# Branch sum by accumulating stores, gate weights in y's memory, last weights in free memory

## The chip, the cores and the metric

One core of one Trainium2 chip runs the kernel. The metric is device time in microseconds for one execution, and less is better. TensorE (PE) multiplies matrices, VectorE (DVE), ScalarE (ACT) and GpSimd (POOL) work on tiles in on-chip memory, and SyncE (SP) issues most of the transfers; each engine runs its own instructions in order and waits for the others through semaphores.

## The reference

One decoder layer with S = D = 1024 and three token mixers side by side:

```python
h = rms_norm(x, g_norm)
proj = h @ w_in            # q, k, v, indexer, latent, cross and gate columns
o_a = dsa_attention(...)   # sparse: indexer scores, the 256 best keys per query, 8 heads of 64
o_b = causal_attention(...)  # latent attention, 8 heads
o_m = cross attention into 256 memory tokens, 4 heads
ys = stack([o_a * silu(z_a), o_b * silu(z_b), o_m * silu(z_m)])
branch = einsum('nbsw,nwd->nbsd', ys, w_branch)
merged = einsum('bsnd,nbsd->bsd', sigmoid(gate_logits), branch)
out = x + merged @ w_out
```

## The kernel before, in words

All products are wanted at fp32 accuracy from faster operands, so each matrix is held as a rounded part and its remainder (hi and lo, names ending in h and l), and each product is three matmuls: `mm3`, lines 273 to 275. Weights come in as a raw tile (name ending in r) by a DMA of SP (`wload`, L258), are cast on ACT (L241), and the remainder is taken on DVE (L244). `hTh` and `hTl` hold the normed, transposed input all the time.

The order of the stages is: projections and norms; cross attention; latent attention; the indexer, which scores keys for the top-k; then the three branches and the output product. The top-k search goes on beside what follows: `run_topk(i_, n)` puts pieces of it on DVE and ACT behind a given instruction. `branch(n, ...)` does one mixer: for four pieces w it makes the z product (`z_part`, 48 matmuls, names z0w for the weights), loads the mixer's output (`osb`), multiplies and splits it into `yh`, `yl`; then for eight column tiles d and two row halves j it makes 12 matmuls into a bank `br`, loads the gate tile `tg` (the tanh that was computed earlier and stored in `s_tg`), and calls `emit`. Branch 2 uses `emit_b`, which stores (tg + 1) * br into the sum `s_acc` in DRAM. Branch 1 uses `emit_m`, which adds to what is there: it loads the tile of `s_acc` first. Branch 0 (`emit_a`, at the end) adds the last part and keeps the sum on chip for the output product.

Around branch 2 and 1 stand `qkv(p)`, p = 0 to 3, which make the sparse attention's queries, keys and values, and `early`, which does three of branch 0's four z products ahead of time and stores them in `s_z`. In the program the order is branch 2 with qkv(0), branch 1 with qkv(1), the first early z, qkv(2), the next, qkv(3), the transposes of head 0's keys (`k_prep`, PE bank `akt`, results `akh`, `akl`), the third early z. Then comes the sparse attention: per head and query group G, `q_prep` transposes queries (bank a_3q for G = 3), the scores go into banks a_3S, softmax gives a_3p, which is transposed (a_3pt) and multiplied with the values (`avst`). Between these a `Filler` runs gate products f_d_j (24 matmuls each, weights f_d_a, result tanh `fo`, stored to `s_tg`). The table PREA says how many products of three matmuls the filler does ahead of the scores of the first units, and what is left runs behind the last unit. Then branch 0 with its last z product (z0w_0, memory pool `w5`), and the output product with weights `wo`, loaded in `pre_wo` at the eighth piece of branch 0.

The order within an engine comes from the tile scheduler. Memory comes from pools that stack on a left and a right side; a new pool that lies in the memory of a closed one makes its first writers wait for the old one's last users.

Of the kernel before, what the change touches and what calls it, by code (L numbers as in the profile page):

```python
# [12 lines left out]
FR = mybir.dt.float32r  # L13
# [3 lines left out]
ALU = mybir.AluOpType  # L17
# [4 lines left out]
S = 1024  # L22
D = 1024
P = 128
# [11 lines left out]
WSB = [1]  # L36
WSI = [1]
PREB = (0, 0, 0, 16)
PREA = (0, 0, 0, 0)
NFQ = 2  # L40
PFQ = 4
NZG = 3
# [53 lines left out]
def f(ap):  # L96
    return ap.bitcast(F32)
# [3 lines left out]
def hybrid_kernel(  # L101
# [5 lines left out]
    nc = tc.nc  # L107
    x, mem, out = x[0], mem[0], out[0]
# [15 lines left out]
    def ps_t(nm, dt=F32):  # L124
        return pp.tile([P, 512], dt, tag="tp", name=nm, bufs=NTP)
# [14 lines left out]
    ident = cp.tile([P, P], F32, name="ident")  # L140
# [475 lines left out]
    with ExitStack() as ph:  # L616
# [31 lines left out]
        with ExitStack() as ph2:  # L648
# [64 lines left out]
            for h in range(4):  # L713
                tp = ps_t(f"kmt{h}")
# [614 lines left out]
    with w3s as ph:  # L1329
# [5 lines left out]
        def acc_at(d, j):  # L1335
            return s_acc[d * P:(d + 1) * P, j * 512:(j + 1) * 512]
# [6 lines left out]

        def emit_m(d, j, tg, pb):
            ac = wk.tile([P, 512], F32, tag="ac", name=f"am{d}_{j}", bufs=3)
            nc.sync.dma_start(ac, acc_at(d, j))
            nc.vector.scalar_tensor_tensor(out=tg, in0=tg, scalar=1.0, in1=pb, op0=ALU.add, op1=ALU.mult)
            i_ = nc.vector.tensor_tensor(ac, tg, ac, op=ALU.add)
            nc.gpsimd.dma_start(acc_at(d, j), ac)
            run_topk(i_, 2.6)  # L1350

        def qkv(p):
# [62 lines left out]
                nc.sync.dma_start(f(qs)[:, 4 * j:4 * j + 4, :],  # L1415
                                  s_qa[p][j].rearrange("p (t h d) -> p t h d", t=4, h=2)[:, :, hh, :])

        def k_prep(p, hh):
            if (p, hh) in st:
                return  # L1420
            h = 2 * p + hh
            kd = st["k", p]
            kTh = hd.tile([P, S], FR, tag="kTh", name=f"akh{h}")
            kTl = hd.tile([P, S], FR, tag="kTl", name=f"akl{h}")
            for j in range(2):
                tp = ps_t(f"akt{h}_{j}")
                for i in range(4):
                    nc.tensor.transpose(tp[:, i * P:(i + 1) * P],
                                        kd[:, 4 * j + i, hh].rearrange("p a d -> p (a d)"), ident)
                cs = slice(j * 512, (j + 1) * 512)  # L1430
                nc.scalar.copy(kTh[:, cs], tp)
                nc.vector.tensor_tensor(kTl[:, cs], tp, f(kTh[:, cs]), op=ALU.subtract)
            st[p, hh] = (kTh, kTl)

        ws[:] = WSG

        def early(a, b):
# [5 lines left out]
        early(0, 1)  # L1443
        qkv(2)
        ys.close()
        hd = hds.enter_context(tc.tile_pool(name="aheads", bufs=2, side="right", reuse_waits="tile"))
        load_k(0)
        load_q(0, 0)
        load_q(0, 1)
        early(1, 2)  # L1450
        qkv(3)
        k_prep(0, 0)
        early(2, NZG)

    run_topk(None, 99)
# [1 line left out]


    with ExitStack() as ph:
        wk2 = ph.enter_context(tc.tile_pool(name="awork2", bufs=2, reuse_waits="tile"))  # L1460
        vp = ph.enter_context(tc.tile_pool(name="avals", bufs=2, reuse_waits="tile"))
        for t in range(2):
            m = msk[t] = vp.tile([P, (t + 1) * P], BF, name=f"msk{t}", bufs=1)
            nc.gpsimd.memset(m, 0.0)
            nc.gpsimd.affine_select(out=m[:, t * P:(t + 1) * P], in_=m[:, t * P:(t + 1) * P],
                                    pattern=[[-1, P]], compare_op=ALU.is_ge, fill=NEG, base=0,
                                    channel_multiplier=1)
        zero_tiles(wk2, 1)
        pv_bufs[:] = PVA

        def load_gen(p):
            yield 1
            if p:
                load_k(p)
            vst = vp.tile([P, NT, 4, 64], FR, tag="vst", name=f"avst{p}")
            st["v", p] = (vst, [None, None])
            for j in range(2):
                nc.sync.dma_start(f(vst).rearrange("p t e d -> p (t e d)")[:, 1024 * j:1024 * j + 1024], s_va[p][j])
            yield 1
            if p:  # L1480
                load_q(p, 0)
            yield 1
            if p:
                load_q(p, 1)

        def q_prep(p, hh, G):
            h = 2 * p + hh
            qs = st["q", p, hh]
            nm = f"a{h}_{G}"
            tp = ps_t(nm + "q", FR)  # L1490
            for b in range(2):
                nc.tensor.transpose(tp[:, b * P:(b + 1) * P],
                                    qs[:, 2 * G + b], identr)
            qT = wk2.tile([P, 256], FR, tag="aqT", name=nm + "qT")
            nc.vector.tensor_copy(qT, f(tp)[:, 0:256])
            return qT

        def s_mm(u, b):
            (p, hh, G), qT = u.unit, u.q
            kTh, kTl = st[p, hh]  # L1500
            t = 2 * G + b
            n = (t + 1) * P
            q_ = qT[:, b * P:(b + 1) * P]
            mx = sm.tile([P, 2], F32, tag="mxb", name=f"{u.nm}mx{b}")
            pt = p_tile(wk2, G, f"{u.nm}p{b}")
            ch = s_chunks(n)
            for c, (k0, w, m) in enumerate(ch):
                sp = ps_s(f"{u.nm}S{b}_{c}")
                nc.tensor.matmul(sp[:, 0:w], q_, kTh[:, k0:k0 + w], start=True, stop=False)
                nc.tensor.matmul(sp[:, 0:w], q_, kTl[:, k0:k0 + w], start=False, stop=True)  # L1510
                masked(pt, sp, m, msk[t][:, k0:k0 + m], k0, mx, c)
            return pt, min_of(mx, ch), n

        def scores(p, hh, G, q):
            u = Scores(f"a{2 * p + hh}_{G}", wk2, G, s_mm)
            u.unit, u.q = (p, hh, G), q
            return u

        def pv(p, hh, G, sc):
            vst, oa = st["v", p]  # L1520
            if oa[hh] is None:
                oa[hh] = wk2.tile([P, S], F32, tag="oa", name=f"oa{p}", bufs=1) if hh == 0 else oa[0]
            o_ = oa[hh]

            def store():
                nc.sync.dma_start(s_o[0][P * p:P * p + P, :], o_)
            return PV(sc.nm, wk2, G, sc, hh, lambda kt: vst[:, kt, 2 * hh:2 * hh + 2].rearrange("p e d -> p (e d)"),
                      o_[64 * hh:64 * hh + 64, 2 * G * P:2 * (G + 1) * P],
                      store if hh == 1 and G == GORD[-1] else None)

        fp = ph.enter_context(tc.tile_pool(name="afill", bufs=1, reuse_waits="tile"))
        ws[:] = WSQ
        attention(load_gen, k_prep, q_prep, scores, pv, pool_filler(fp, take_jobs("F", NFA), FWA, FBB), PFA, PREA, GENA, LDA)

# [4 lines left out]
    with ExitStack() as ph:  # L1539
# [6 lines left out]
        wpa = ph.enter_context(tc.tile_pool(name="w6a", bufs=1, reuse_waits="tile"))  # L1546
        with ExitStack() as ph2:
            wkz = ph2.enter_context(tc.tile_pool(name="zwork5", bufs=2, reuse_waits="tile"))
            wpool = ph2.enter_context(tc.tile_pool(name="w5", bufs=2, reuse_waits="tile"))
            yp = ph2.enter_context(tc.tile_pool(name="y5", bufs=1, reuse_waits="tile"))  # L1550
            wk = ph2.enter_context(tc.tile_pool(name="gwork5", bufs=2, reuse_waits="tile"))

            def emit_a(d, j, tg, pb):
                ac = wk.tile([P, 512], F32, tag="ac", name=f"ac{d}_{j}", bufs=3)
                nc.sync.dma_start(ac, s_acc[d * P:(d + 1) * P, j * 512:(j + 1) * 512])
                i_ = nc.vector.scalar_tensor_tensor(out=tg, in0=tg, scalar=1.0, in1=pb, op0=ALU.add, op1=ALU.mult)  # L1556
                split_low(i_)
                nc.gpsimd.tensor_tensor(ac, ac, tg, op=ALU.add)  # L1558
                nc.scalar.activation(hTh[d][j], ac, AF.Copy, scale=0.25)
                late.append((d, j, ac))  # L1560

            late = []

            def split_low(after):
                for d, j, ac in late:
                    with tc.issue_after(after.ins) if after is not None else ExitStack():
                        nc.vector.scalar_tensor_tensor(out=hTl[d][j], in0=ac, scalar=0.25, in1=f(hTh[d][j]),
                                                       op0=ALU.mult, op1=ALU.subtract)
                late.clear()

            assert all((0, d) in gates_done for d in range(NK))
            pool_raw[:] = PRF
            pre = []

            def pre_wo(after, pe):
                pre.append(0)
                if len(pre) == PRW:
                    pool_raw[:] = [1, 8]
                    wo_load(wpa, 0)
                    pool_raw[:] = list(PRF)  # L1580

            ws[:] = WSF
            branch(0, C_ZA, wpool, wkz, yp, s_o[0], emit_a, pre_wo, 4, wk, ZB5, OB5)
            ws[:] = WSO
            split_low(None)
# [44 lines left out]
```

## Time and profile before

| what | value |
|---|---|
| three runs | 1434.66, 1435.96, 1440.41 us, median 1435.96 |
| profiled execution | 1439.17 us, span 1437.4 us, mean granted clock of PE 0.987 |
| PE busy | 1369.2 us, 95% of the span, 7440 matmul rows |
| DVE busy | 965.6 us, 67% |
| ACT busy | 680.8 us, 47% |
| POOL busy | 200.7 us, 14% |

The span is the time between the first and the last instruction of the profiled execution. Busy shares say how much of it an engine worked; a wait row says which engine waited at which line and what came last before it went on; a window row gives the busy time of all engines between two times, with the clock that PE was granted as a share of full speed.

### The profile page before, as it was taken

The numbers are of one execution on the slowest core, as the hardware profiler recorded it, in microseconds if no ns is written. First come the engines' busy times: TensorE is split into PE (matmuls) and PEld (weight loads), VectorE is DVE, ScalarE is ACT, GpSimd is POOL, SyncE is SP. The second block draws the span as 40 slices with busy tenths as digits, with TensorE's granted clock in tenths as the row PEclk, the third lists the DMA queues.
The fourth block names the chain that finished last, engine by engine and source line by source line (L and its number), as shares of the span: only waits on it lengthen the run. The fifth ranks groups of instructions, "written<-read, shape, count | busy, mean of one in ns | idle before, by whom it ended". The sixth has DMA issues, their size and how long they took to land.

```text
span 1437.4 us, 20940 instructions
## 1 busy us (share of the span) xinstructions
PE 1369.2 (95%) x7440; PEld 1171.5 (82%) x7440; DVE 965.6 (67%) x2450; ACT 680.8 (47%) x1464; POOL 200.7 (14%) x240
## 2 busy tenths in 40 slices
PE   7999999899999999999999999799889999969998
PEld 5998888788988889877897897598878888857787
DVE  5845436678888751688868787877778788836411
ACT  6635433366666651465645554333246566623200
POOL 3050004510102000000022003112300000003200
PEclk9999999999999999999999999999999999989999
DMA  7411212311121130112408523853163341266622
GB/s 247 132 45 59 92 37 86 116 54 41 49 68 40 45 126 23 30 44 81 132 37 271 153 74 138 282 153 125 52 183 97 95 125 60 73 191 186 208 97 73
DMA packets 155992, 151.65 MB, mean 106 GB/s; under 512 B 38256, under 2 KB 115056, under 8 KB 155888
## 3 DMA queue, kind: packets, MB, share of 16 engines
q1 hardware_dynamic: 149328, 127.77, 29.9%
q0 software_dynamic: 5984, 20.45, 3.7%
q10 hardware_dynamic: 576, 2.10, 0.4%
q8 instruction: 58, 0.95, 0.3%
q14 instruction: 46, 0.38, 0.1%
HBM read 103.63 MB, written 46.66 MB: 105 GB/s over the span
## 4 chain that ended last, share of the span: by engine, by line
PE 59%; DVE 14%; issue 8%; DMA 7%; ACT 7%; POOL 3%; SPq 0%; ACTq 0%; DVEq 0%; POOLq 0%
PE f L273 5%; PE f L274 5%; PE f L275 5%; DVE kdj L1039 3%; ACT kag L1045 2%; PE o L275 2%; PE o L273 2%; PE o L274 2%; DVE idx L1233 1%; DMA s_acc<-am 1%; PE ixps L274 1%; PE ixps L275 1%; PE ixps L273 1%; PE b_3pt L462 1%; PE qmps L275 1%
## 5 line engine op out<-in xcount | busy, mean ns | idle before, releaser
L1045 ACT ACTIVATE kag<-idx,kaT 128x896 bf16<-128x896 f32 (+2 forms) x96 | 82.8, 862 | 51.2 <-DVE kaT L1066 44.9
L1039 DVE TENSOR_SCALAR_CACHE_REDUCE kdj<-idx,kdT 128x1024 bf16<-128x1024 f32 (+2 forms) x96 | 92.3, 962 | 0.7
L273 PE MATMUL f<-hTh,f_0h 128*128 128x512 f32 x184 | 78.8, 428 | 2.6 <-ACT fo L365 1.9
L273 PE MATMUL f<-hTh,f_1h 128*128 128x512 f32 x184 | 76.4, 415 | 0.0
L275 PE MATMUL f<-hTh,f_0l 128*128 128x512 f32 x184 | 74.1, 403 | 0.0
L275 PE MATMUL f<-hTh,f_1l 128*128 128x512 f32 x184 | 74.0, 402 | 0.0
L274 PE MATMUL f<-hTl,f_1h 128*128 128x512 f32 x184 | 73.8, 401 | 0.0
L274 PE MATMUL f<-hTl,f_0h 128*128 128x512 f32 x184 | 73.7, 400 | 0.0
L1558 POOL TENSOR_TENSOR ac<-ac,tg 128x512 f32<-128x512 f32 x16 | 22.2, 1397 | 277.9 <-DVE tg L1556 264.3
L1600 DVE TENSOR_TENSOR xr<-o,xr 128x512 f32<-128x512 f32 x16 | 11.1, 691 | 65.1 <-PE o L275 64.2
L1227 ACT ACTIVATE irl<-is 128x512 f32<-128x512 f32 (+1 forms) x80 | 37.8, 528 | 15.6 <-DVE idx L1233 11.9
L365 ACT ACTIVATE fo<-f 128x512 f32<-128x512 f32 x48 | 28.8, 599 | 33.9 <-PE f L275 30.0
L273 PEld LDWEIGHTS f<-hTh,f_0h 128*128 128x128 f32 x184 | 34.8, 189 | 9.5 <-ACT fo L365 4.1
L1233 DVE SCALAR_TENSOR_TENSOR idx<-irl,wi,idx 128x1024 f32<-128x1024 f32 (+5 forms) x42 | 40.3, 959 | 2.6 <-ACT irl L1227 0.9
L275 PEld LDWEIGHTS f<-hTh,f_0l 128*128 128x128 f32 x184 | 35.0, 190 | 6.4
L275 PEld LDWEIGHTS f<-hTh,f_1l 128*128 128x128 f32 x184 | 34.8, 189 | 6.3
L274 PEld LDWEIGHTS f<-hTl,f_1h 128*128 128x128 f32 x184 | 34.9, 190 | 4.5
L273 PEld LDWEIGHTS f<-hTh,f_1h 128*128 128x128 f32 x184 | 34.9, 189 | 4.2
L274 PEld LDWEIGHTS f<-hTl,f_0h 128*128 128x128 f32 x184 | 35.1, 191 | 3.8
L1225 PE MATMUL is<-kih,iqT 128*128 128x512 f32 (+1 forms) x80 | 30.1, 381 | 2.8 <-ACT irl L1227 2.4
L273 PE MATMUL z<-hTh,z0w_0h 128*128 128x512 f32 x40 | 18.2, 456 | 13.2 <-ACT z0w_0h L241 9.2
L1174 DVE TENSOR_SCALAR wi<-ixps 128x8 f32<-128x8 f32 x8 | 1.3, 166 | 42.0 <-ACT xi L1172 42.0
(1238 smaller groups left out, 4772.9 us busy)
## 6 DMA issues: line engine op xcount, KB each, us to landing
s_tg<-fo SPq DMA_DIRECT2D x48, 256.0 KB, 2.0
tg<-s_tg SPq DMA_DIRECT2D x48, 256.0 KB, 3.9
f_0r<-in_w_in_dram SPq DMA_DIRECT2D x23, 256.0 KB, 3.0
f_1r<-in_w_in_dram SPq DMA_DIRECT2D x23, 256.0 KB, 3.0
xx<-in_x_dram SPq DMA_DIRECT2D x8, 512.0 KB, 7.2
osb<-s_o SPq DMA_DIRECT2D x16, 256.0 KB, 3.1
s_acc<-ab POOLq DMA_DIRECT2D x16, 256.0 KB, 5.0
am<-s_acc SPq DMA_DIRECT2D x16, 256.0 KB, 4.0
```

Source lines behind the costliest of these rows:

```text
L273: nc.tensor.matmul(ps, ah, bh, start=start, stop=False)
L274: nc.tensor.matmul(ps, ah, bl, start=False, stop=False)
L275: nc.tensor.matmul(ps, al, bh, start=False, stop=stop)
L365: nc.scalar.activation(o, ps, AF.Tanh, scale=0.5)
L462: nc.tensor.transpose(tp[:, i, :], Pt[b][:, kt * P:(kt + 1) * P], ident)
L1039: nc.vector.tensor_scalar(out=junk, in0=idx[t], scalar1=T[:, i:i + 1], scalar2=0.0, op0=ALU.is_ge, op1=ALU.add, accum_out=cnt[:, i:i + 1])
L1045: nc.scalar.activation(junk, idx[t], AF.Sign, bias=T[:, i:i + 1], accum_out=cnt[:, i:i + 1])
L1225: nc.tensor.matmul(sp[:, 0:w], q_, kih[:, k0:k0 + w], start=True, stop=False)
L1227: nc.scalar.activation(rl[:, k0:k0 + m], sp[:, 0:m], AF.Relu)
L1233: i_ = nc.vector.scalar_tensor_tensor(out=acc[:, 0:n], in0=rl[:, 0:n], scalar=wc, in1=acc[:, 0:n], op0=ALU.mult, op1=ALU.add)
L1558: nc.gpsimd.tensor_tensor(ac, ac, tg, op=ALU.add)
L1600: nc.vector.tensor_tensor(xr, ps, xr, op=ALU.add)
```

## The change

Three things change. `emit_m` writes (tg + 1) * br into its tile and stores it with `accum_op=ALU.add`, issued by POOL as before, without loading `s_acc`. The filler's pool `afill` moves to the right side, into the memory of branch 1's `y`, which is closed after qkv(2); PREA becomes (0, 0, 4, 4); and the transposed keys of the sparse attention move from the pool `aheads` to a new one, `akeys`, which exists only from the attention on, so that head 0's `k_prep` is not called ahead of it. In the last stage `gwork5` is allocated ahead of `w5` and `y5`, so that `w5` and `y5` lie further along on the left side.

```diff
-PREA = (0, 0, 0, 0)
+PREA = (0, 0, 4, 4)
...
         def emit_m(d, j, tg, pb):
             ac = wk.tile([P, 512], F32, tag="ac", name=f"am{d}_{j}", bufs=3)
-            nc.sync.dma_start(ac, acc_at(d, j))
-            nc.vector.scalar_tensor_tensor(out=tg, in0=tg, scalar=1.0, in1=pb, op0=ALU.add, op1=ALU.mult)
-            i_ = nc.vector.tensor_tensor(ac, tg, ac, op=ALU.add)
-            nc.gpsimd.dma_start(acc_at(d, j), ac)
+            i_ = nc.vector.scalar_tensor_tensor(out=ac, in0=tg, scalar=1.0, in1=pb, op0=ALU.add, op1=ALU.mult)
+            nc.gpsimd.dma_start(acc_at(d, j), ac, accum_op=ALU.add)
             run_topk(i_, 2.6)
...
         ys.close()
+        fp = hds.enter_context(tc.tile_pool(name="afill", bufs=1, side="right", reuse_waits="tile"))
         hd = hds.enter_context(tc.tile_pool(name="aheads", bufs=2, side="right", reuse_waits="tile"))
...
         qkv(3)
-        k_prep(0, 0)
         early(2, NZG)
...
     with ExitStack() as ph:
+        kp2 = ph.enter_context(tc.tile_pool(name="akeys", bufs=2, reuse_waits="tile"))
         wk2 = ph.enter_context(tc.tile_pool(name="awork2", bufs=2, reuse_waits="tile"))
...
+        def k_prep(p, hh):
+            h = 2 * p + hh
+            kd = st["k", p]
+            kTh = kp2.tile([P, S], FR, tag="kTh", name=f"akh{h}")
+            kTl = kp2.tile([P, S], FR, tag="kTl", name=f"akl{h}")
...
-        fp = ph.enter_context(tc.tile_pool(name="afill", bufs=1, reuse_waits="tile"))
         ws[:] = WSQ
...
             wkz = ph2.enter_context(tc.tile_pool(name="zwork5", bufs=2, reuse_waits="tile"))
+            wk = ph2.enter_context(tc.tile_pool(name="gwork5", bufs=2, reuse_waits="tile"))
             wpool = ph2.enter_context(tc.tile_pool(name="w5", bufs=2, reuse_waits="tile"))
             yp = ph2.enter_context(tc.tile_pool(name="y5", bufs=1, reuse_waits="tile"))
-            wk = ph2.enter_context(tc.tile_pool(name="gwork5", bufs=2, reuse_waits="tile"))
```

SP's queue in the middle of branch 1's products (am is the tile of the sum, b1w the branch's weights, tg the gates), before with - and after with +:

```order
-L1318 DMA tg_1_1_9766<-s_tg_100 128x512
-L1318 DMA tg_2_0_9794<-s_tg_100 128x512
-L1346 DMA am_1_9781<-s_acc 128x512
+L1318 DMA tg_1_1_9760<-s_tg_100 128x512
 L258 DMA b1w5r<-in_w_branch_dram 128x4x128
-L1318 DMA tg_2_1_9827<-s_tg_100 128x512
-L1346 DMA am_0_9809<-s_acc 128x512
+L1318 DMA tg_2_0_9786<-s_tg_100 128x512
+L1318 DMA tg_2_1_9817<-s_tg_100 128x512
 L258 DMA b1w6r<-in_w_branch_dram 128x4x128
```

The loads of am are gone, and gates and weights follow one another directly; so it goes through the whole branch.

PE at the start of the sparse attention, before (head 0's keys were transposed ahead of z_2; akt here is head 1):

```order
L275 MATMUL z_2_1_11183<-hTh_1_143,z0w_4l 128x512
L1492 MATMUL a_3q<-identr,aqs_0_10651 128x128 x2
L1428 MATMUL akt_0_11299<-ident,akd_10646 128x128 x4
L1428 MATMUL akt_1_11306<-ident,akd_10646 128x128
L1509 MATMUL a_3S_0_11252<-akh_11130,a_3qT 128x512
L1510 MATMUL a_3S_0_11252<-akl_11131,a_3qT 128x512
L1509 MATMUL a_3S_1_11256<-akh_11130,a_3qT 128x384
```

The same place now; ahead of these rows stand z_2, eight transposes of head 0's keys, 12 matmuls of f_0_0, a_3q and nine more of f_0_0:

```order
L273 MATMUL f_0_0_11227<-hTh_0_142,f_0_1h 128x512
L274 MATMUL f_0_0_11227<-hTl_0_158,f_0_1h 128x512
L275 MATMUL f_0_0_11227<-hTh_0_142,f_0_1l 128x512
L1506 MATMUL a_3S_0_11263<-akh_11199,a_3qT 128x512
L1507 MATMUL a_3S_0_11263<-akl_11200,a_3qT 128x512
L1506 MATMUL a_3S_1_11267<-akh_11199,a_3qT 128x384
L1507 MATMUL a_3S_1_11267<-akl_11200,a_3qT 128x384
L273 MATMUL f_0_1_11272<-hTh_1_129,f_0_0h 128x512
```

A whole gate product, 24 matmuls, stands ahead of the first scores, and f_0_1 is spread between the next ones. Behind the last attention unit 15 matmuls of the filler are left, where there were 39.

SP's queue at the end of the attention, before (fo are the gate results, wo the output weights, z0w_0 the last z weights):

```order
L1526 DMA s_o_95<-oa_13318 128x1024
L366 DMA s_tg_99<-fo_7_0_13919 128x512
L258 DMA wo_0r<-in_w_out_dram 128x2x512
L366 DMA s_tg_99<-fo_7_1_13947 128x512
L258 DMA wo_1r<-in_w_out_dram 128x2x512
L258 DMA z0w_0r<-in_w_in_dram 128x8x128
L1300 DMA osb_3_0_14035<-s_o_95 128x512
L1300 DMA osb_3_1_14043<-s_o_95 128x512
L1300 DMA osb_0_0_14053<-s_o_95 128x512
```

And now:

```order
L258 DMA z0w_0r<-in_w_in_dram 128x8x128
L258 DMA b0w0r<-in_w_branch_dram 128x4x128
L366 DMA s_tg_99<-fo_7_0_13855 128x512
L258 DMA b0w1r<-in_w_branch_dram 128x4x128
L1318 DMA tg_0_0_14095<-s_tg_99 128x512
L1551 DMA ac_0_14110<-s_acc 128x512
L1523 DMA s_o_95<-oa_13317 128x1024
L1318 DMA tg_0_1_14115<-s_tg_99 128x512
L1551 DMA ac_1_14130<-s_acc 128x512
L366 DMA s_tg_99<-fo_7_1_13918 128x512
L1300 DMA osb_3_0_14007<-s_o_95 128x512
L1300 DMA osb_3_1_14015<-s_o_95 128x512
```

z0w_0r and the first two branch weights now stand ahead of the last two gate stores; wo_0r comes four rows behind this piece, after the fourth osb, and wo_1r, wo_2r and wo_3r among the loads of branch 0.

## Rows read from the trace of the kernel before

**Rows 1.** The page, busy time, share and instructions of each engine, whole span:

```profile
PE 1369.2 (95%) x7440; PEld 1171.5 (82%) x7440; DVE 965.6 (67%) x2450; ACT 680.8 (47%) x1464; POOL 200.7 (14%) x240
```

**Rows 2.** Waits of PE, whole span: line waited, releaser, us in total, times, longest:

```profile
PE z L273 <- ACT z0w_0h L241: 9.2, 1, 9.2
...
PE br L273 <- DVE tg L1347: 4.9, 2, 3.3
PE z L273 <- DVE tg L1347: 4.0, 1, 4.0
...
PE br L273 <- ACT yh L1305: 3.4, 1, 3.4
PE akt L1428 <- DVE a_1v L1386: 3.0, 1, 3.0
PE br L273 <- DVE ab L1340: 2.5, 2, 1.4
```

**Rows 3.** Windows: stretch, length, busy PE, PEld, DVE, ACT, POOL; clock, DMA share, GB/s:

```profile
742.00:792.00 50.00, 46.49 (x199) 36.77 (x198) 40.35 (x122) 27.92 (x61) 14.11 (x22) 1.00 0.61 203
880.00:930.00 50.00, 39.41 (x157) 30.66 (x158) 40.74 (x107) 20.18 (x41) 13.03 (x20) 0.96 0.77 249
930.00:934.00 4.00, 4.00 (x13) 3.14 (x13) 3.12 (x8) 1.88 (x5) 0.54 (x1) 0.66 0.95 307
1031.00:1036.00 5.00, 4.44 (x15) 3.68 (x16) 4.12 (x15) 2.72 (x9) 1.04 (x2) 0.66 0.14 56
1053.00:1057.00 4.00, 4.00 (x23) 3.70 (x23) 2.40 (x7) 1.87 (x4) 0.00 (x0) 0.67 1.21 293
1277.00:1281.00 4.00, 3.79 (x8) 2.58 (x9) 1.23 (x1) 0.32 (x2) 0.00 (x0) 0.51 0.83 258
1310.00:1347.00 37.00, 36.58 (x155) 28.35 (x155) 22.11 (x32) 10.89 (x18) 17.26 (x14) 1.00 0.70 216
```

**Rows 4.** Waits, branch 1's products, 880 to 935 us, columns as in rows 2:

```profile
DVE am L1348 <- DMA am<-s_acc: 7.3, 7, 1.9
```

**Rows 5.** Chain of waits, 885 to 932 us: start, us, what:

```profile
890.07 6.26 DMA s_acc<-am
896.35 3.64 DMA am<-s_acc
```

**Rows 6.** Groups of instructions, 880 to 930 us: busy, mean ns, idle before:

```profile
L1348 DVE TENSOR_TENSOR am<-tg,am 128x512 f32<-128x512 f32 x14 | 9.7, 690 | 7.4 <-DMA am<-s_acc 7.3
L1347 DVE SCALAR_TENSOR_TENSOR tg<-tg,br 128x512 f32<-128x512 f32 x14 | 9.5, 680 | 0.0
```

**Rows 7.** DMA issues, 742 to 932 us: count, KB each, median us to landing:

```profile
am<-s_acc SPq DMA_DIRECT2D x15, 256.0 KB, 4.0
s_acc<-am POOLq DMA_DIRECT2D x14, 256.0 KB, 4.2
```

**Rows 8.** Waits of PE, first scores, 1049 to 1056 us:

```profile
PE a_0S L1509 <- DVE a_0qT L1495: 2.2, 1, 2.2
PE a_3pt L462 <- DVE a_3p L519: 1.5, 1, 1.5
```

**Rows 9.** DMA issues, sparse attention, 1040 to 1258 us:

```profile
avst<-s_va SPq DMA_DIRECT2D x8, 512.0 KB, 5.1
```

**Rows 10.** Timeline of SP's queue, 1258 to 1295 us: start, us, what:

```profile
1268.89 0.32 SPq L366 DMA_DIRECT2D s_tg<-fo  x1
1269.65 0.38 SPq L258 DMA_DIRECT2D wo_1r<-in_w_out_dram  x1
1270.13 0.46 SPq L258 DMA_DIRECT2D z0w_0r<-in_w_in_dram  x1
```

**Rows 11.** Groups of instructions, 1262 to 1350 us, columns as in rows 6:

```profile
L273 PE MATMUL br<-yh,b0w6h 128*128 128x512 f32 x8 | 3.2, 403 | 0.3 <-ACT b0w6h L241 0.3
...
L244 DVE TENSOR_TENSOR wo_1l<-wo_1r,wo_1h 128x1024 fp32r<-128x1024 f32 x1 | 1.2, 1226 | 5.8 <-ACT wo_1h L241 5.8
...
L241 ACT CAST wo_1h<-wo_1r 128x1024 fp32r<-128x1024 f32 x1 | 1.0, 1044 | 5.5 <-DMA wo_1r<-in_w_out_dram 5.5
```

More of the change, by code (lines that the diff above doesn't have):

```diff
@@ L1416, in load_q @@
                                   s_qa[p][j].rearrange("p (t h d) -> p t h d", t=4, h=2)[:, :, hh, :])
[L1418 to L1433, printed above, removed]
         ws[:] = WSG
@@ L1469, in hybrid_kernel @@
         pv_bufs[:] = PVA
+        def k_prep(p, hh):
[3 more added lines that the diff above has]
+            kTl = kp2.tile([P, S], FR, tag="kTl", name=f"akl{h}")
+            for j in range(2):
+                tp = ps_t(f"akt{h}_{j}")
+                for i in range(4):
+                    nc.tensor.transpose(tp[:, i * P:(i + 1) * P],
+                                        kd[:, 4 * j + i, hh].rearrange("p a d -> p (a d)"), ident)
+                cs = slice(j * 512, (j + 1) * 512)
+                nc.scalar.copy(kTh[:, cs], tp)
+                nc.vector.tensor_tensor(kTl[:, cs], tp, f(kTh[:, cs]), op=ALU.subtract)
+            st[p, hh] = (kTh, kTl)
         def load_gen(p):
```

## The prediction, made before the changed kernel ran

> **What bounds the kernel now.** I read the busy shares first: TensorE (PE) is busy 95% of the span [rows 1], so a change can only win what PE idles, or what it loses at a lower clock. The total doesn't say where that is, so next come the longest waits of PE [rows 2]. Look for those that lie after 860 us, where the change is: 9.2 us in front of the last z product, 4.9 us inside branch 1's products and 4.0 us at the first z product behind them, 3.4 us at the start of branch 0's products, 3.0 us at the key transposes of head 0. Then the windows [rows 3]: what to see there is the granted clock behind such a gap. In four microseconds after the branch-1 gap it is 0.66, at the start of the sparse attention 0.66 and 0.67, after the 9.2 us gap 0.51; where PE had not idled it is 1.00, so each long gap is paid twice. The last row of [rows 3] gives the pace at full clock: 155 matmuls in 36.58 us, 0.236 us each, 2.83 us for a tile of 12 in the branch stages and 0.71 us for a product of three. Everything below is priced with these.
>
> **Part 1, emit_m.** Removed: 16 loads of 256 KB from SP's queue and 16 adds on DVE. The adds are 14 of 0.690 us in the stage's window beside 14 of 0.680 for the instruction that stays [rows 6]: 11 us for 16. DVE is busy 40.74 of 50 us there [rows 3], and blocks 7.3 us more, waiting for the am loads [rows 4]: 48 of 50 us, so DVE set the pace of this stage. The chain shows why the loads are late [rows 5]: a load must wait for the store that last used its buffer. A store of 6.26 us, a load of 3.64 us, the add and the next issue are about 11 us for one turn of three buffers, 3.7 us a tile against 2.83 for PE.
>
> After the change a turn is the landing L of the accumulating store plus the 0.68 us instruction, the issue of the store and the hand-overs, 1.5 us as an estimate: (L + 1.5)/3 a tile, hidden behind PE up to L = 7.0 us. No row shows an accumulating store. The near end is the plain store of the same tile, median 4.2 us; the far ends are store and load one after the other, 4.2 + 4.0 = 8.2 us by the medians [rows 7] and 6.26 + 3.64 = 9.9 us by the longest pair [rows 5]. I take some 6 us: a read within the transfer costs less than a second transfer with its own start, and then no PE wait comes from it. What goes is 4.9 + 4.0 us of waits [rows 2] and 4.00 x 0.34 = 1.4 us of clock [rows 3], 10.3 us. What comes back is what the same form shows in branch 2, whose emit_b already stores without load and add: 2.5 us of waits on DVE [rows 2]. Net 8 us. At L = 8.2 the 13 tiles behind the first three would wait 13 x (3.23 - 2.83) = 5 us, net 5; at 9.9 it is 13 x 0.97 = 12.6, a loss of 2. Upper end 11 (all waits go, and the weights of the next stage, which SP issues behind the am loads, come sooner).
>
> The 0.77 DMA share and 249 GB/s of this stage [rows 3] leave a second question. The Trainium skill, "DMA: Bandwidth & Descriptors", section "Rules for kernel authors", states that an accumulating DMA reads its destination and writes it later, so the engines still carry the bytes of the removed load; and this speaks against the change. No row before shows it; counted so, a tile still moves 0.875 MiB, at 2.83 us 324 GB/s, and with the 307 GB/s of [rows 3] as the most, the stage would take 0.16 us a tile longer, 2.5 us in all: by the page part 1 gives 5.5, not 8.
>
> **Part 2, gate products ahead of the scores.** The same 24 matmuls move from behind the last attention unit to its start, so PE's work is unchanged; what counts is what they cover. In the order, z_2 now follows the last qkv matmul directly, the key transposes come behind z_2, and 24 matmuls (5.7 us) stand between the transposes, a_3q and the scores. Gone are the 3.0 us wait of the transposes for DVE [rows 2] with its dip, 4.44 x 0.34 = 1.5 us [rows 3], and the 2.2 and 1.5 us waits at a_0S and a_3pt [rows 8] with 4.00 x 0.33 = 1.3 us: 9.5. z_2 needs a bank too, but the z_1 product behind the third qkv follows without a listed wait, so I expect the same of z_2. Upper end 10. Lower end 4: the 3.0 us and its dip reappear at z_2. The three first gate-weight tiles are loaded and split earlier, in the third qkv stage: three casts and three subtractions of some 0.6 and 0.7 us beside PE work; and the first avst loads now wait for the stores whose memory they take. They are needed only at the first value product, behind the 24 matmuls, so I cost them at nothing; without that cover they would be a wait of up to the 5.1 us of such a transfer [rows 9]. Value taken: 9. What is late next is the chain of softmax behind the first scores, which now runs under f_0_1.
>
> **Part 3, the last weights.** Before, z0w_0r is issued at 1270.13, behind the last gate store and wo_1r in SP's queue [rows 10], because its memory comes free only when the fillers end; that store, at 1268.89, ends PE's work, and PE waits 9.2 us [rows 2], then runs at 0.51, 3.79 x 0.49 = 1.9 us lost [rows 3]. After, z0w_0r stands ahead of the last two gate stores, and b0w0r, b0w1r and the first tg and ac loads too; the leftover of 15 matmuls (3.5 us) runs straight into the z product. Gain 11. The 3.4 us at the start of branch 0's products stays: it is the tail tanh, multiply, cast behind the last z product, which nothing shortens.
>
> Given back: the four wo pieces, 512 KB each, were loaded and split while PE idled or ran z. Now wo_0r is issued behind the first osb loads, and wo_1r to wo_3r beside branch 0's own loads; their splits, 1.05 us on ACT and 1.2 us on DVE each [rows 11], stand between those of b0w. The b0w tiles have one raw buffer: load, cast and subtraction of tile d+1 must end within two tiles, 5.66 us, and already b0w6 misses it by 0.3 us on PE [rows 11]. Three pieces in that stage delay single tiles by one or two of these splits: 1 to 7 us, I take 4. DVE and ACT are busy 22 and 11 of 37 us there [rows 3], which covers the rest. Net 7, ends 4 and 11.
>
> **Sum.** 8 + 9 + 7 = 24 us. The profiled execution took 1439.17 us (span 1437.4), 3.2 us above the median of the runs, so 1415 on its own scale and 1436 - 24 = 1412 on that of the median, 1.7% less. A measurement of this kernel tells about 0.5% (7 us) from no change.
>
> **Rivals.**
> - *The accumulating store is slow.* The place is the three am buffers. The price is 13 x ((L + 1.5)/3 - 2.83); it eats part 1 at L = 9.4 and all three parts from L = 13. At 16 us it costs 39 us against 26 gained: 1449, slower. For it: no row has such a store, and POOL's queue carries it alone. Against: the longest plain pair is 9.9 us. Chance 0.06.
> - *Part 1 halves*, by L of 8 to 10 us or by the bytes that stay on the DMA engines (the rule above): part 1 gives -2 to 5, 1415 to 1422, about 1418. For it: 0.95 of the DMA engines busy at 930 us [rows 3]. Against: branch 2 runs with 0.61 and 203 GB/s. Chance 0.18.
> - *Branch 0 starves*: the wo pieces hold its weights and all of the 11 us in front go again: 1419. For it: the one raw buffer and [rows 11]. Against: idle ACT and DVE. Chance 0.18.
> - *The start of the attention keeps its first wait*, at z_2: 5 us less, 1417. Chance 0.10.
> - *Two or three of these at once*, or top-k work that DVE no longer does in branch 1's gaps runs later and stops PE there: within 7 us of before, about 1432. Chance 0.06.
> - The forecast: 0.42.
>
> **How the numbers follow.** Faster by over 0.5% is the forecast and the middle three, 0.88; same 0.06; slower 0.06. All three upper ends, 11 + 10 + 11, give 1404, with half the 3.4 us of [rows 2] 1402; the range ends at 1428, past the three middle rivals and two of them together, which leaves out the slow store and the last case.
>
> **What would show it.** Part 1: no L1346 row, the waits of br on DVE under 3 us in 880 to 930, clock 1.00 behind it, and a landing of the accumulating stores under 7 us; a landing over 9.4 and waits as before would make it wrong. Part 2: z_2 directly behind qkv without a wait, no dip around the first scores, f_0_0 ahead of a_3S; wrong if a wait of 2 to 3 us stands in front of z_2 or of the first value product. Part 3: z0w_0h done before the last a_1o, no wait at z, clock 1.00 there, and the gap before br still some 3.4 us; wrong if branch 0's products show waits for b0w or wo pieces that sum to over 7 us. The prediction as a whole fails if the stages before 880 us differ by more than a microsecond or two, since nothing moves there.

## The result

The changed kernel took 1425.26 us in the median of five runs (1423.71 to 1430.6), the kernel before 1438.46 in five runs beside them: a ratio of 0.9915, 95% interval 0.9885 to 0.9944, some 12 us less. The time lies in the range, the sign is right, the size is half of the 24 us that were forecast. The profiled execution of the changed kernel is its slowest run, 1430.6 us with a span of 1428.8, so the traces show 8.6 us of difference and the runs 12 to 13.

The page after, busy times, DMA queues and HBM traffic:

```profile
PE 1370.9 (96%) x7440; PEld 1173.3 (82%) x7440; DVE 954.4 (67%) x2434; ACT 681.4 (48%) x1464; POOL 209.3 (15%) x240
...
q1 hardware_dynamic: 147024, 123.58, 29.0%
q0 software_dynamic: 7008, 20.45, 4.8%
...
HBM read 99.43 MB, written 46.66 MB: 102 GB/s over the span
```

The same DMA lines of the page before:

```profile
q1 hardware_dynamic: 149328, 127.77, 29.9%
q0 software_dynamic: 5984, 20.45, 3.7%
...
HBM read 103.63 MB, written 46.66 MB: 105 GB/s over the span
```

DVE lost its 11 us of adds [rows 1]. The first line fell from 29.9% of 1437.4 to 29.0% of 1428.8, 15.4 us of the DMA engines' time less without the loads; the second rose from 3.7% to 4.8%, also 15.4 us more, for the same bytes stored. The shares are rounded, so each difference can be 1.4 us off. The Trainium skill, "DMA: Bandwidth & Descriptors", section "Rules for kernel authors", says that an accumulating DMA reads its destination too; the engines' time agrees (it is not less than before), while the page's HBM bytes read fall by 4.2 MB, the 16 loads.

Waits of PE after, 870 to 1350 us (in total, times, longest):

```profile
PE a L273 <- DVE a_0v L1384: 7.0, 2, 5.8
PE br L275 <- DVE b0w2l L244: 4.4, 1, 4.4
PE br L273 <- ACT yh L1305: 3.9, 1, 3.9
PE a L274 <- DVE a3w3l L244: 3.8, 1, 3.8
PE f L273 <- DVE sz L1270: 2.8, 1, 2.8
```

Windows after (length, busy PE, PEld, DVE, ACT, POOL, clock, DMA share, GB/s):

```profile
880.00:930.00 50.00, 47.33 (x195) 37.57 (x196) 37.04 (x102) 23.19 (x47) 18.93 (x22) 0.97 0.93 223
930.00:934.00 4.00, 4.00 (x21) 3.55 (x20) 2.79 (x7) 1.61 (x2) 0.85 (x1) 1.00 0.98 178
...
970.00:980.00 10.00, 10.00 (x42) 9.26 (x43) 6.12 (x21) 1.89 (x6) 4.41 (x6) 0.80 0.33 131
...
990.00:1000.00 10.00, 6.16 (x27) 5.84 (x26) 6.80 (x16) 2.99 (x6) 4.18 (x7) 0.83 0.63 209
1043.00:1048.00 5.00, 4.95 (x12) 3.89 (x13) 1.78 (x3) 0.61 (x2) 2.55 (x9) 0.50 0.55 210
1264.00:1268.00 4.00, 4.00 (x19) 3.11 (x18) 0.00 (x0) 0.60 (x1) 0.00 (x0) 1.00 0.89 287
...
1299.00:1303.00 4.00, 3.79 (x9) 3.02 (x10) 2.40 (x2) 0.76 (x2) 1.28 (x1) 0.50 0.79 242
```

DMA issues after, 742 to 932 us (KB each, median us to landing):

```profile
s_acc<-ab POOLq DMA_DIRECT2D x16, 256.0 KB, 5.1
s_acc<-am POOLq DMA_DIRECT2D x16, 256.0 KB, 6.2
```

Every wait that the prediction wanted to remove is gone: the 4.9 and 4.0 us of branch 1, the 3.0 us at the transposes, the 9.2 us at z0w_0h [rows 2], the 2.2 and 1.5 us at the first scores [rows 8]. PE is busy 47.33 of 50 us in branch 1, where it was 39.41 [rows 3]. But others stand in their place: 5.8 us at a_0v in the third qkv, 3.8 at a3w3l (2.3 before), 2.8 at the first gate product (the row of sz), 4.4 at b0w2l, each with a low clock behind: 0.80 and 0.83 over ten microseconds, 0.50 and 0.50 over five and four (0.50 is the lower of the two levels).

A table over all combinations of the three parts shows where, each from one profiled execution. It takes from each PE timeline the start of four matmuls: the first product with b1w1 in branch 1, the first of the third qkv (A is the time between them), the first of z_2 (B), the first of branch 0's products (C), the first of the output product (D). From there to the end every kernel takes 93.5 us.

| kernel | A | B | C | D | sum with 93.5 |
|---|---|---|---|---|---|
| before | 66.1 | 90.0 | 261.7 | 50.0 | 561.3 |
| part 1 | 56.2 | 94.8 | 261.4 | 49.1 | 555.0 |
| part 2 | 66.4 | 89.5 | 251.6 | 52.9 | 554.0 |
| part 3 | 66.1 | 89.7 | 256.9 | 48.9 | 555.1 |
| 1 + 2 | 55.3 | 94.5 | 252.9 | 52.5 | 548.7 |
| 1 + 3 | 54.9 | 94.3 | 257.3 | 47.8 | 547.8 |
| 2 + 3 | 65.3 | 89.3 | 248.5 | 55.5 | 552.0 |
| the change (1 + 2 + 3) | 55.5 | 95.8 | 251.1 | 56.1 | 552.1 |

### The profile page after: what moved, and what is told of

Read it like the earlier page. It is cut to its first block, busy times and chain, and to the rows that moved or that the text cites. A ratio compares the mean times of both kernels' runs of the same rounds, so it can differ in the third digit from the quotient of the medians.

```text
span 1428.8 us, 20870 instructions
## 1 busy us (share of the span) xinstructions
PE 1370.9 (96%) x7440; PEld 1173.3 (82%) x7440; DVE 954.4 (67%) x2434; ACT 681.4 (48%) x1464; POOL 209.3 (15%) x240
## 4 chain that ended last, share of the span: by engine, by line
PE 64%; DVE 13%; ACT 6%; issue 6%; DMA 5%; POOL 3%; SPq 0%; ACTq 0%; DVEq 0%; POOLq 0%
PE f L273 6%; PE f L274 5%; PE f L275 5%; DVE kdj L1039 2%; PE o L274 2%; PE o L273 2%; PE o L275 2%; PE br L275 2%; PE br L273 2%; ACT kag L1045 2%; PE br L274 2%; DVE idx L1233 1%; PE ixps L274 1%; PE ixps L275 1%; PE ixps L273 1%
## 5 line engine op out<-in xcount | busy, mean ns | idle before, releaser
L1554 POOL TENSOR_TENSOR ac<-ac,tg 128x512 f32<-128x512 f32 x16 | 25.0, 1565 | 265.2 <-DVE tg L1552 257.3
L1270 DVE SCALAR_TENSOR_TENSOR sz<-sz,z 128x512 f32<-128x512 f32 x24 | 16.3, 683 | 23.4 <-ACT sz L1269 23.4
```

Of the source, the lines that this page charges most:

```text
L1270: zi[0] = nc.vector.scalar_tensor_tensor(out=sz, in0=sz, scalar=1.0, in1=pz[j], op0=ALU.add, op1=ALU.mult)
```

## The experiments

The ratios are to the kernel before, run beside each. Two runs of one program can differ by 5 us, so single steps of 2 or 3 us are read from the stage that was touched, not from the total.

**Each part alone.** Part 1 alone is the diff of `emit_m`, part 3 alone that of the pools' order; for part 2 these two are taken back. 

> The kernel before with the accumulating store of branch 1 alone. Theory A (the three parts are independent, and what part 1 won was lost between 930 and 970 us because splits of the early gate weights stood in VectorE's queue): without those splits part 1 keeps its gain, 9 to 11 us faster than before, and TensorE's wait for a_0v at the third qkv stays under 1.5 us. Theory B (the top-k chain on VectorE sets the time up to 995 us, whatever branch 1 does): 0 to 3 us faster, and the last weight piece of the fourth qkv (a3w3l) is done at about 994 us as before.

 

> The kernel before with the gate weights in y's memory and eight products ahead of the scores alone. Theory A: 3 to 5 us are won around 1030 to 1060 us, and the three early splits cost 0 to 3 us of it in the third qkv, where VectorE in the kernel before is late anyway: 0 to 4 us faster. Theory B: the splits cost nothing, 4 to 8 us faster.

 

> The kernel before with the new place of the last stage's memory alone. Theory A (the wo pieces move into branch 0 and hold its weights): the 9.2 us wait for z0w_0h goes with its 1.9 us of low clock, a wait of 4 to 5 us for b0w2l with its own low clock comes: 3 to 6 us faster. Theory C (the wait for b0w2l comes from the other two parts, which shift the attention against the loads): no such wait, 9 to 11 us faster.

Measured: part 1 1432.39 us, ratio 0.9946 (0.9930 to 0.9962); part 2 1431.93, 0.9942 (0.9926 to 0.9958); part 3 1431.73, 0.9941 (0.9925 to 0.9956). About 8 us each, and 24 together, where the whole gives 12. The waits of PE from 870 to 1350 us, part 2 alone:

```profile
PE br L273 <- ACT yh L1305: 7.1, 1, 7.1
...
PE br L275 <- DVE b0w2l L244: 3.2, 1, 3.2
PE f L273 <- DVE sz L1270: 2.8, 1, 2.8
```

part 3 alone:

```profile
PE br L273 <- ACT yh L1305: 10.8, 1, 10.8
```

and part 1 alone:

```profile
PE z L273 <- ACT z0w_0h L241: 9.0, 1, 9.0
...
PE a L274 <- DVE a3w3l L244: 3.8, 1, 3.8
```

The wait for z0w_0h stands in neither part 2's nor part 3's rows. Part 2 moves the fillers' weights away from the memory in which z0w lies, part 3 moves z0w away from theirs; either does it: z0w_0r, issued at 1270.13 before [rows 10], is issued at 1257.91 with part 2 alone and at 1239.44 with part 3 alone.

In part 3's trace 7 us of the gain reappear at yh. ACT's timeline there shows what stood in front of it:

```profile
1274.35 1.05 ACT L241 CAST wo_1h<-wo_1r 128x1024 fp32r<-128x1024 f32 x1 [6.59 <-DMA wo_1r<-in_w_out_dram]
1275.30 0.59 ACT L1269 ACTIVATE sz<-z 128x512 f32<-128x512 f32 x1
...
1280.49 1.04 ACT L241 CAST wo_2h<-wo_2r 128x1024 fp32r<-128x1024 f32 x1 [1.74 <-DMA wo_2r<-in_w_out_dram]
1281.44 0.59 ACT L1269 ACTIVATE sz<-z 128x512 f32<-128x512 f32 x1
```

PE ended the two halves of the last z product at 1271.54 and 1277.12; each tanh comes some 4 us later, behind a wo cast that waits for its load. In the changed kernel the second tanh starts 0.04 us behind its half. No run moves the wo pieces in part 3 alone, so this is read from the order and not tested.

Theory A of part 1 was right that A keeps the gain, but not on the cause of the loss behind it: B is 94.8 here too, with no early split in DVE's queue. Its theory B (nothing gained) fell. For part 2 the 8 us are at the upper end of theory B, though neither theory names the z0w_0h wait that went. For part 3 the 8 us lie between A and C; there is no wait for b0w2l, as C says, and the loss stands at yh instead.

**Two parts at a time.** 

> The changed kernel with branch 1's load and add put back, so parts 2 and 3 without part 1. Alone, parts 2 and 3 were worth 8 us each, and each trace alone no longer has the wait for z0w_0h. Theory D (both remove that same 9 us wait, so it is counted twice): the two together are 7 to 10 us faster than before. Rival E (they are independent, and the loss in the whole comes from part 1): 15 to 17 us faster.

 

> The kernel before with parts 1 and 3, without the gate weights in y's memory. Theory D (part 1 loses its gain only where the gate-weight splits stand in the third qkv): 14 to 17 us faster than before, so at least as fast as the whole change. Rival E: parts 1 and 3 also take from each other, 9 to 12 us faster.

 

> The kernel before with parts 1 and 2, without the new place of the last stage's memory. Theory D (part 3 adds nothing where part 2 already frees the memory of the last z weights): within 2 us of the whole change, 11 to 14 us faster than before. Rival E: 6 to 9 us less gain than the sum of the two alone gives, and part 3 is worth 5 us or more on top.

Measured: 2 + 3 1430.74 us, 0.9957 (0.9938 to 0.9976), 6 us where the two alone gave 17; 1 + 3 1424.28, 0.9922 (0.9896 to 0.9948); 1 + 2 1423.74, 0.9914 (0.9885 to 0.9944). Theory D holds for 2 + 3 and for 1 + 2: parts 2 and 3 overlap almost wholly (gain of C and D together: 7.2 us for 2, 5.9 for 3, 7.7 for both), and part 1 with either is as fast as all three. For 1 + 3 its 14 to 17 us missed: 11 is in rival E's range. In the table C and D of the whole are even worse than those of 1 + 3 by 2 us.

**The third gate weight held back.** `self.act` is the tanh of the first gate product:

```diff
                     if j == 1 and i + 1 < len(self.jobs):
-                        w = self.load(*self.jobs[i + 1])
+                        with tc.issue_after(self.act.ins) if (n, d) == (0, 0) else ExitStack():
+                            w = self.load(*self.jobs[i + 1])
...
-                    nc.scalar.activation(o, ps, AF.Tanh, scale=0.5)
+                    self.act = nc.scalar.activation(o, ps, AF.Tanh, scale=0.5)
```

> The changed kernel with the cast of the third gate-weight tile (f_1_0) queued behind the tanh of the first gate product, so that its split leaves the third qkv stage. Theory A: the 5.8 us wait for a_0v shrinks to 1 to 3 us, 4 to 7 us faster than the changed kernel, about 1419 to 1422 where before is 1438. Theory B: the top-k chain holds the stage anyway, within 2 us of the changed kernel.

The reason to try it are DVE's waits after, 930 to 1000 us:

```profile
DVE z0w_0l L244 <- ACT z0w_0h L241: 5.6, 1, 5.6
DVE f_0l L244 <- ACT f_0h L241: 2.8, 1, 2.8
...
DVE ar_1rp L422 <- POOL a_1xq L1389: 2.3, 1, 2.3
```

and this piece of DVE's timeline there, where f_0l (here the third weight tile, f_1_0) keeps the top-k and a_0ss, a_0xk, a_0v behind it:

```profile
958.60 0.16 DVE L1065 TENSOR_SCALAR kdr<-kdc 128x3 int32<-128x3 f32 x1
961.52 0.69 DVE L244 TENSOR_TENSOR f_0l<-f_0r,f_0h 128x512 fp32r<-128x512 f32 x1 [2.76 <-ACT f_0h L241]
...
965.59 0.41 DVE L1378 TENSOR_REDUCE a_0ss<-asq 128x4 f32<-128x256 f32 x1
...
969.42 0.28 DVE L1384 TENSOR_TENSOR a_0v<-a,a_0v 128x128 fp32r<-128x128 f32 x1
```

Measured: 1425.32 us, 0.9896 (0.9879 to 0.9913); the 5.8 us wait at a_0v is gone, B is 92.1 instead of 95.8. The total is some 3 us better by the ratios, whose intervals overlap, so theory A is borne out in the stage and only likely in the total. Other kernels with all early splits in place waited 3.2 to 4.5 us there, so 5.8 is a high value of one execution; two further kernels with the split held waited 1.7 and 3.1.

**Keys and queries loaded later.** `load_k(0)`, `load_q(0, 0)`, `load_q(0, 1)` behind `early(1, 2)`, on top of the held kernel. 

> The changed kernel with the third gate-weight tile held back (as in the earlier run) and, besides, the loads of head 0's keys and queries issued behind the second early z product instead of ahead of it. From the third qkv's first matmul to a3w3l the kernel before takes 52.1 us, part 1 alone 56.5, part 2 alone 55.4, the changed kernel 62.4, the held one 58.9. Theory G (VectorE stands at z0w_0l for 5.6 us, because eight loads of keys and queries hold SP's queue, and at the gate splits): this stretch comes down to 53 to 56 us, the whole 3 to 6 us faster than the held kernel. Theory H (the stretch is set by the last weight pieces a3w2 and a3w3, whose buffers come free with the third qkv): 58 us or more, within 2 us of it.

Measured: 1423.8 us, 0.9900 (0.9878 to 0.9921); B 92.7. Theory G fell: DVE's 5.6 us at z0w_0l are gone, but it waits 3.4 us at z0w_4l and 3.4 at f_0l instead, and the stretch to a3w3l is 59.2 us, as it was (58.9).

**The queries' scaling behind their rotation.** The last row of DVE's waits above, 2.3 us for GpSimd's scaled a_1xq, stands in DVE's queue ahead of a3w3l.

```diff
-                nc.gpsimd.tensor_tensor(xq, xq, rr[:, :, 0:2]..., op=ALU.mult)
                 for e, v in enumerate((xk, xq)):
                     rope(...)
+                nc.gpsimd.tensor_tensor(xq, xq, rr[:, :, 0:2]..., op=ALU.mult)
```

> The changed kernel with the queries' scaling on GpSimd moved behind their rotation (the same product in another order, in all four qkv stages), so that VectorE's rotation no longer waits for GpSimd. Theory M (the 2.3 us wait ahead of a3w3l in VectorE's queue keeps TensorE waiting 3.85 us there): that wait of TensorE falls to 1 to 2.5 us, and the whole is 2 to 6 us faster, since the same wait stands in the other three stages too. Theory H (the buffers of a3w3 come free too late): TensorE's wait stays over 3 us, and nothing is gained.

Measured: 1419.33 us, 0.9853 (0.9830 to 0.9876), 6 us below the changed kernel's median. The waits of PE, 870 to 1350 us:

```profile
PE a L273 <- DVE a_0v L1384: 5.9, 1, 5.9
...
PE a L274 <- DVE a3w3l L244: 1.9, 1, 1.9
```

The wait at a3w3l fell from 3.8 to 1.9, and the stretch from the third qkv to it from 62.4 to 56.5 us, which is theory M; but a wait of 5.9 at a_0v stands in the fourth qkv now, and B as a whole is 95.5. The gain is in C (245.8), where the 2.8 us wait at the first gate product is gone. So M is right on the wait it named, and not on the stage.

**z products out of the gate products' bank**, on the held kernel: `BANKS[2]` from 'fms' to 'ms'. 

> The held kernel with the z products kept out of the PSUM bank that the gate products use. In the changed kernel the first gate product waits 2.85 us for the evacuation of the last z product from that bank. Theory: that wait goes, with some low clock behind it, 2 to 5 us faster than the held kernel. Rival: with two banks fewer turns the z products wait for their own evacuations or VectorE, nothing gained.

Measured: 1421.21 us, 0.9878 (0.9855 to 0.9901), 2.6 us below the kernel with the late loads, run beside it. No wait of f for sz is left, C falls from 252.9 to 247.1. The theory holds in the stage; the gate products now wait 3.0 us in all for their own results, where it was 1.0.

**Branch 0's weights.** Three edits, all on the changed kernel. First the wo pieces, loaded from `emit_a(2, 0)` on with their casts behind that tile's; then two raw buffers, `PRF = (2, 5)`; then six split buffers, `PRF = (1, 6)`. 

> The changed kernel with the wo pieces loaded from the third column tile of branch 0 on and their casts queued behind that tile's cast. Theory D (the wo pieces hold yh and b0w2 in the queues of SP, ACT and VectorE): the 4.4 us wait for b0w2l goes with its low clock, 4 to 7 us faster than the changed kernel. Rival F (the z part and the loads of osb and sz set that time): within 2 us of it.

 

> The changed kernel with two raw buffers instead of one for the weights of the last stage. From the first product of branch 0 to the first output product the kernel before takes 50.0 us, part 3 alone 48.9, the changed kernel 56.1, and 56.2 with the wo pieces moved back. Theory J (one raw buffer makes each b0w tile wait behind its forerunner's split, and the wo pieces only show it): 48 to 51 us, 5 to 7 us faster than the changed kernel. Theory K (the splits on ACT and VectorE stand in the wrong order, whatever the buffers): 54 us or more, within 2 us of it.

 

> The changed kernel with six instead of five buffers for the split weights of the last stage. Theory L (five buffers hold b0w0, b0w1 and the cast of b0w2, so that b0w2l can be written only after the last reader of b0w0h, and then stands behind the tiles' work in VectorE's queue): the 4.4 us wait for b0w2l goes with its low clock, branch 0's products fall from 56 to 49 to 51 us, 4 to 6 us faster than the changed kernel. Theory K (the order of the wo splits alone): another wait of 3 us or more stands in the same stretch, within 2 us of it.

| kernel | median us | ratio (interval) | D |
|---|---|---|---|
| changed | 1425.26 | 0.9915 (0.9885 to 0.9944) | 56.1 |
| wo later | 1425.31 | 0.9923 (0.9895 to 0.9952) | 56.2 |
| two raw buffers | 1424.30 | 0.9902 (0.9879 to 0.9925) | 53.3 |
| six split buffers | 1420.05 | 0.9860 (0.9834 to 0.9885) | 48.8 |

With wo later the wait for b0w2l is gone, and the loss stands elsewhere, at b0w5:

```profile
PE br L275 <- DVE b0w5l L244: 2.0, 1, 2.0
PE br L273 <- ACT b0w5h L241: 1.6, 1, 1.6
```

With two raw buffers it stays:

```profile
PE br L275 <- DVE b0w2l L244: 4.7, 1, 4.7
```

With six split buffers no wait for a weight over 1.1 us is left:

```profile
PE br L273 <- ACT yh L1305: 6.0, 1, 6.0
...
PE br L273 <- ACT b0w4h L241: 1.1, 1, 1.1
```

So theory D of the wo pieces fell (the total is F's), J fell, and L holds: five buffers hold both halves of b0w0 and b0w1 and the cast of b0w2, and b0w2l waits for the last reader of b0w0h. In the kernel before it then stood directly behind the first tile's instruction, and a product of PE released it:

```profile
1304.33 0.68 DVE L1556 SCALAR_TENSOR_TENSOR tg<-tg,br 128x512 f32<-128x512 f32 x1
1305.70 1.24 DVE L244 TENSOR_TENSOR b0w2l<-b0w2r,b0w2h 128x512 fp32r<-128x512 f32 x1 [0.69 <-PE br L274]
```

In the changed one wo_2l, three more tiles and three hTl pieces stood between the two, as DVE's timeline after shows:

```profile
1290.07 0.69 DVE L1552 SCALAR_TENSOR_TENSOR tg<-tg,br 128x512 f32<-128x512 f32 x1 [0.74 <-PE br L275]
1290.67 1.22 DVE L244 TENSOR_TENSOR wo_2l<-wo_2r,wo_2h 128x1024 fp32r<-128x1024 f32 x1
...
1297.86 0.69 DVE L1563 SCALAR_TENSOR_TENSOR hTl<-ac,hTh 128x512 fp32r<-128x512 f32 x1 [1.22 <-ACT hTh L1555]
1298.47 0.69 DVE L244 TENSOR_TENSOR b0w2l<-b0w2r,b0w2h 128x512 fp32r<-128x512 f32 x1
```

**Is part 3, or part 2, needed?** The late-load kernel with part 3 undone, and 1 + 3 with six buffers. 

> The kernel of the late key and query loads without the new place of the last stage's memory (part 3 undone). If part 2 alone frees the last z weights (theory D), this is as fast as that kernel or 1 to 4 us faster, because branch 0's products took 52.5 us with part 2 alone and 56 with both. If part 3 adds something of its own there, it is 3 us slower or more.

 

> Parts 1 and 3 without part 2, with six buffers for the split weights of the last stage. If part 2 wins only what part 3 wins too, this is as fast as the changed kernel with six buffers, within 2 us; if part 2 has a share of its own (the start of the attention), it is 3 us slower or more.

Measured: without part 3 1424.73 us, 0.9905 (0.9881 to 0.9930), against 1423.8 with it: the same. Without part 2 1423.21, 0.9882 (0.9857 to 0.9907), against 1420.05 with all three and six buffers: 3 us slower. So no gain of part 3 is seen where part 2 is, and part 2's own share is about 3 us once branch 0 is not starved, with intervals that overlap. The second table below puts these 3 us behind the attention, where the wait at yh is 10.9 us without part 2 and 6.0 with it, and not at its start.

**Together**: hold, bank, six buffers and scaling. 

> Everything that helped together: the changed kernel with the third gate-weight tile held back, the z products out of the gate products' bank, six buffers in the last stage and the queries' scaling behind the rotation. If the causes are as stated and separate, 5 us from the bank and the hold, 5 from the buffers and 2 to 6 from the scaling: 1410 to 1414. If they share waits: 1415 to 1418.

Measured: 1416.13 us, ratio 0.9832 (0.9810 to 0.9854), by the ratio 24 us below before (1441.39 beside it), faster than both kernels. By its ratio it would stand at 1414 beside a before of 1438, at the lower of the two expectations' edge; as measured it is the higher. No wait of PE for a gate bank is left, and none for a weight of branch 0 over 1.1 us:

```profile
PE br L273 <- ACT yh L1306: 7.6, 2, 6.2
PE a L273 <- DVE a_0v L1385: 3.8, 1, 3.8
PE a L274 <- DVE a3w3l L244: 1.9, 1, 1.9
```

## Why the prediction was half right

A second table cuts B and C anew, at the last attention matmul: E runs from the first matmul of the third qkv to it, F from it to the first of branch 0's products. Where the gate product is moved ahead of the scores, its 24 matmuls, 5.7 us, are taken off E and put to F, so that the rows can be compared.

| kernel | E | F | D |
|---|---|---|---|
| before | 316.4 | 35.3 | 50.0 |
| part 1 | 321.0 | 35.2 | 49.1 |
| part 2 | 312.9 | 28.3 | 52.9 |
| part 3 | 315.4 | 31.3 | 48.9 |
| 1 + 2 | 319.3 | 28.1 | 52.5 |
| 1 + 3 | 320.5 | 31.1 | 47.8 |
| 2 + 3 | 313.1 | 24.7 | 55.5 |
| the change | 322.3 | 24.6 | 56.1 |
| the change, hold and bank | 315.5 | 24.9 | 54.5 |
| the change, six buffers | 319.5 | 26.6 | 48.8 |
| 1 + 3, six buffers | 319.5 | 31.4 | 46.9 |

**Part 1, 8 us.** The store's landing was taken as some 6 us, a choice between 4.2 and 8.2 to 9.9 without a row of its own, and is 6.2; 7.0 was the point from which PE would wait, and it does not. Of 10.3 removed, A shows 9.9 for part 1 alone, 10.6 in the whole; of the 2.5 that were to come back PE waits 0.6. (The nets given for slower landings, 5 and a loss of 2, leave these 2.5 out.) The step that failed is the one behind it, "net 8 us": nothing was set against it in the stages after. B lengthens by 4 to 6 us in every kernel with part 1 as the program stood (94.3 to 95.8 against 89.3 to 90.0), whichever of the other parts is there: PE arrives earlier at a_0v, a3w2 and a3w3 than DVE delivers them. Of the wait at a3w3l half is shown to be DVE's wait for GpSimd; the held split took 3.7 us off B in one execution, the late loads nothing more. Neither they nor the moved scaling bring B back to 90, so what sets B stays open. Part 1 is worth 5 to 7 us by the traces of 1, 1 + 2 and 1 + 3, none by those of 2 + 3 and the whole (the fastest of ten executions and the slowest of five), and 3 to 8 by the ratios.

**Part 2, 9 us.** This is the term that failed. The waits it named went, 3.0, 2.2 and 1.5 us with their dips. But E, where the 9 us had to stand, is only 3.6 us shorter with part 2 alone, 2.2 on top of part 3 and 1.7 on top of part 1; in the whole it is 1.8 longer than in 1 + 3. Two things that were costed at nothing took the gain back. "z_2 needs a bank too": z_2 did start without a wait, but the gate product behind it needs the bank that z_2 holds, and waits 2.8 us with 0.50 of the clock for five microseconds after it, 2.5 us more. The three early casts and subtractions were put "beside PE work", but what counts on an engine that runs in order is what they wait for: one stood 2.8 us at the front of DVE's queue with the top-k and the qkv work behind it. With the bank changed and that split held, E is 315.5, 5.5 us below part 1 alone; the other 4 of the 9.5 stay open.

**Part 3, 7 us, and the sum.** The wait at z0w_0h went with its low clock, and F is 10.6 us shorter, where 11 were taken. The wait at yh is 3.9 us, near the 3.4 that were to stay: the tail is as the prediction has it, and 0.3 us of DVE's wait for a stored z piece came on top. What came back in branch 0 is 4.4 us and half the clock in 3.79 us, 6.3 us, where 4 was taken and 7 the end. Its cause is another than the text has: not the one raw buffer but the five split ones.

That parts 2 and 3 overlap is no fault of the sum, which counts the wait at z0w_0h once, under part 3. What is incomplete is the reason "its memory comes free only when the fillers end": part 2 takes the fillers out of that memory, so it frees z0w_0 by itself. Of the 8 us that part 2 alone measured, 4 are that wait (F shorter by 7.0, D longer by 2.9), not those it was made for. 16 us for parts 2 and 3 were 6 (ratio) to 9 (trace, sum of the stages): of the 7 to 10 that are missing, some 6 belong to E and 2 to branch 0.

**The rivals.** The slow store did not come: 6.2 us against a threshold of 9.4. "Branch 0 starves" (1419) and "the start of the attention keeps its first wait" (1417) came together, the second as another wait. The case of two or three at once was given 0.06, with 1432; at 1425 it was milder, and it is what happened. Its other form, top-k work that runs later, is not the cause: between the third qkv and z_2 DVE's rows of the top-k (names that begin with ka and kd) sum to 38.3 us in the whole and 38.5 in part 1 alone, where they were 37.4. What the Trainium skill says of the destination's read agrees with the engines' time, yet the 2.5 us worked out from it did not show: PE waited 0.6 us for DVE at the end of branch 1, at a DMA share of 0.93.

## What to carry to other kernels

When several edits go in together, ask of each wait which of them removes it alone: a wait can be won once, and edits that each look like 8 us may be one edit. A product that is moved in to cover a wait needs a bank where it lands: here it waited 2.8 us for one. A split or cast that is loaded ahead costs little beside its place in an in-order queue, and the price of that place is the wait for its data, which falls on everything behind it. Before a producer is blamed for a late weight, count the buffers against the pieces that must be alive: one buffer more took 7 us from its stage here, where moving the load took none.

## What the runs showed of the hardware

An accumulating store of 256 KB landed in 6.2 us where the plain one took 4.2 [rows 7] and branch 2's plain ones in the same trace 5.1, and 16 of them used some 15 us more of the DMA engines' time, as much as the 16 loads that they replaced. Its issue takes POOL longer, which the groups of 880 to 935 us show, after:

```profile
L1347 POOL DMA_DIRECT2D s_acc<-am x16 | 13.7, 859 | 30.8 <-DVE am L1346 16.3 <-DVE kar L1065 9.6 <-DVE kdT L1066 4.4
```

and before:

```profile
L1349 POOL DMA_DIRECT2D s_acc<-am x15 | 8.1, 540 | 37.4 <-DVE am L1348 24.7 <-DVE kar L1065 7.3 <-DVE kdT L1066 3.1
```

859 ns against 540; no wait of PE for POOL came of it here, with POOL busy 18.93 of 50 us. Executions of one program differed by 5 us and more, and the first matmul of branch 1 with b1w1, ahead of which the three parts change no more than that branch's first tiles, started between 872.8 and 877.4 us in the eight kernels of the first table, so a change of less than 1% is read from its stages here.
